# Two-layer hybrid backbone, feed-forward stages: weight halves split on GpSimd instead of ScalarE, operands and rests made on VectorE instead of GpSimd, products put in another order, and every second weight block kept in another pool of tiles

## The chip, the cores and the metric

The kernel runs on one core of a Trainium2 chip. The time is that of one execution in device microseconds (us), the median of several runs. The engines are called PE (TensorE, matmul; PEld is its weight load), DVE (VectorE), ACT (ScalarE), POOL (GpSimd) and SP (the engine that issues most DMAs). L246 is line 246 of the kernel.

## The reference, cut to what matters

```python
D_MODEL, SEQ, CTX_LEN, DEPTH, FFN_HIDDEN = 1024, 1024, 256, 2, 4096
def squared_relu_mlp(h, w1, w2):
    return jnp.square(jax.nn.relu(h @ w1)) @ w2
for l in range(DEPTH):
    need_ctx = l < DEPTH - 1
    m_lat = silu(c) @ w_mod[l] + b_mod[l]             # six rows of 1024, as m_ctx from c_ctx
    sh1, sc1, ga1, sh2, sc2, ga2 = split(m_lat, 6)
    pl = modulate(rms_norm(x, g_mix[l]), sh1, sc1) @ w_in[l]      # pc from ctx likewise
    ...                                               # four groups of mixers: SSD, RG-LRU, two attentions
    x = x + ga1 * (concat(ya, yb, yc, yd) @ w_out[l])
    x = x + ga2 * squared_relu_mlp(modulate(rms_norm(x, g_ffn[l]), sh2, sc2), w_ffn1[l], w_ffn2[l])
    if need_ctx:
        ctx = ...                                     # the same for the 256 context tokens
return x
```

All of it is float32. The latent tokens are 1024 rows, the context 256; layer 1 computes no context output.

## The kernel before, in words

Activations lie transposed: a tile holds 128 features by tokens. The tokens come in three groups, the context (256) and two latent groups of 512 (`G_CTX`, `G_LAT`). A float32 product is made of three fp32r matmuls (`mm3`, L141 to L143): high by high, high by low, low by high. So every operand is split: the high part is a rounding copy (`copy_a` on ACT, L130), the low part the difference (a subtraction on POOL, L246). Weights come through `wsplit` in halves of 128x512: SP issues the DMA of `raw` (L258, two buffers for the halves), ACT writes half of `wh`, POOL half of `wl` (three buffers each), and the next DMA into that `raw` waits for POOL.

The first feed-forward product (FFN1, 32 blocks of 128 hidden features; block `fc`) is done over two by two quarters of the latent half with seven quarter products in place of eight. `quarter` makes operands for that from the second latent group. `hidden_first` runs for an even block the context (layer 0 alone) and the first latent group, for an odd block the context alone. In the first latent group of an even block, four of eight steps of k make one quarter product; ACT copies it out of PSUM into `r` (L130) and sends it to DRAM, and then the other four steps are added in the same PSUM bank. `quarter` runs woven into `hidden_first`. `hidden_rest` takes 16 steps `q`, each with five quarter products of 12 matmuls, called `y` with w2, c21, m5, c12 and m7, c21 and c12 one step late. `weights(q)` loads two tiles `u` of 128x1024, makes sums and differences on DVE (L1300 to L1303), the high parts on ACT and the low parts on POOL (L1306, L1309). The second product (FFN2, in `ffn`) takes blocks in pairs, with 48 matmuls for each latent group and the context.

`mod_bank` computes a third of the modulation of a layer (`w_mod`, 8 MB): for each of 8 steps k two halves `raw` are loaded, and after each half two matmuls of 32 rows by 512 go to their own 32 columns of the array (L316). Bank 0 of layer 0 runs at the start, banks 1 and 2 of a layer beside its mixers (with `E` tiles, three buffers, as `land`), bank 0 of layer 1 in FFN2 of layer 0.

`weave` merges such streams by costs that the streams yield, and a scheduler then orders the instructions of each engine. Each engine runs its own in order, and waits on semaphores.

Of the kernel before, what the change touches and what calls it, by code (L numbers as in the profile page):

```python
# [93 lines left out]
class Net:  # L94
# [210 lines left out]
    def mod_bank(self, l, b, land, tag="po"):  # L305
# [3 lines left out]
        for k in range(KD):  # L309
            for hf in range(2):  # L310
                raw = f(land())[:, :1024]
                c0 = 2048 * b + 1024 * hf
                nc.sync.dma_start(raw, self.I["w_mod"][l, k * P:(k + 1) * P, c0:c0 + 1024])
                for q in range(2):
                    cg = 2 * hf + q
                    nc.tensor.matmul(ps[32 * cg:32 * cg + 32, :], self.csil[:, 2 * k:2 * k + 32], raw[:, 512 * q:512 * q + 512],  # L316
                                     start=k == 0, stop=k == KD - 1, skip_group_check=True,
                                     tile_position=(0, 32 * cg))
                yield 0.9
# [884 lines left out]
    def quarter(self, h, t, x, l, t0, rs):  # L1204
# [12 lines left out]
        def row(k):  # L1217
            a = self.S(n)
            self.stt(a, x.at(k, t0, n), p["s"][1][:, k, 0:1], rb, ALU.mult, ALU.mult)
            self.act(a, a, AF.Identity, bias=p["mods"][:, 24 + k, 0:1])  # L1220
            return a
        for k2 in range(0, 4, 2):
            rows = [(k, row(k), row(k + 4)) for k in (k2, k2 + 1)]
            yield 2.0
            for k, b12, b22 in rows:
# [4 lines left out]
                nc.gpsimd.tensor_sub(t3, b22, b12)  # L1230
# [18 lines left out]
    def hidden_first(self, l, h, groups):  # L1249


        hh, hl = h
        w1 = self.I["w_ffn1"][l]
        tags = ("pm", "qk", "qk")
        for fc in range(0, FFN // P, 1 if len(groups) == 3 else 2):
            wh, wl = self.next_weights()[0] if self.wq or self.ready else self.wcols(w1, fc * P)
            for (t0, n) in (groups[:-1] if fc % 2 == 0 else groups[:1]):
                ps = self.PS(self.pick(tags))[:, :n]
                for k in range(KD):
                    c = slice(k * P, k * P + P)  # L1260
                    self.mm3(ps, wh[:, c], wl[:, c], hh.at(k, t0, n), hl.at(k, t0, n), k == 0,
                             k in (3, KD - 1), True)
                    if k % 2:
                        yield n * 2 * 3 * 216e-3 / 512
                    if k == 3 and t0 >= CTX:
                        r = self.B()
                        self.copy_a(r, ps)
                        self.nc.scalar.dma_start(self.part[fc // 2], r)
                self.squared(self.B(n), fc, t0, n, ps)

    def hidden_rest(self, l, h, t):
# [11 lines left out]
        def weights(q):  # L1283
            raws = []
            for j in range(2):
                r = self.U()[:, :1024].rearrange("p (k c) -> p k c", k=4)
                nc.sync.dma_start(r, w1[512 * j:512 * j + 512, 256 * q:256 * q + 256].rearrange("(k p) c -> p k c", p=P))
                raws.append(r)
# [20 lines left out]
            nc.gpsimd.tensor_sub(lo[4].rearrange("p (k c) -> p k c", k=4), a(1, 1), f(h4))  # L1309
# [316 lines left out]
```

## Time and profile before

| | |
|---|---|
| median of 3 runs | 3211.46 us (3209.78 to 3217.77) |
| the profiled execution | 3211.08 us, of which the span of the trace is 3209.3 us |
| FFN1 of layer 0, from about | 845 us into the span, `hidden_first` to 1072, `hidden_rest` to 1300 |
| FFN2 of layer 0 | 1300 to 1780 us |
| FFN1 of layer 1 | `hidden_first` to 2588 us, `hidden_rest` to 2815 |
| FFN2 of layer 1 | from 2815 us |

The page gives the busy time of each engine over the span. Busy time of PE is modelled (a matmul of 128x512 shows 0.39 us, while the next one starts 0.23 us later), so its share is near 100% wherever it doesn't wait. The stages are told from the names of what is read.

### The profile page before, as it was taken

How to read it: one execution, taken by the hardware profiler on the slowest of the kernel's cores; microseconds unless marked ns; L12 is line 12 of the kernel's file. 1: busy time of each engine (PE TensorE's matmuls, PEld its weight loads, DVE VectorE, ACT ScalarE, POOL GpSimd, SP SyncE). 2: the span in 40 equal slices, each digit the busy share in tenths (PEclk: the TensorE clock that was granted, in tenths of full speed). 3: DMA queues.
4: the chain of work that ended last, by engine and by line, in shares of the span. 5: the costliest groups of instructions: out<-in, count | busy, mean ns of one | idle time of the engine just before them, and what ended most of it. 6: DMA issues, size and time to landing. Idle time of an engine off the chain costs nothing.

```text
span 3209.3 us, 46000 instructions
## 1 busy us (share of the span) xinstructions
PE 3033.6 (95%) x16354; PEld 2481.0 (77%) x16354; DVE 2078.0 (65%) x4143; ACT 1573.0 (49%) x3668; POOL 1087.8 (34%) x916
## 2 busy tenths in 40 slices
PE   6998998989978999999999999999999899999998
PEld 4788887778767777888888688787777677777776
DVE  5787777777640344677665777778787544467664
ACT  4575776666454444312111576676675644432111
POOL 2214123232584454222112512223333764522220
PEclk8999999999999999999999999999999999999999
DMA  8300012321334545633222400112322454452221
GB/s 308 93 17 24 22 36 81 128 94 42 130 122 139 177 145 168 221 128 102 86 81 64 153 18 17 27 42 85 116 79 101 147 189 149 158 175 90 95 69 70
DMA packets 239830, 335.97 MB, mean 105 GB/s; under 512 B 37360, under 2 KB 157296, under 8 KB 239600
## 3 DMA queue, kind: packets, MB, share of 16 engines
q1 hardware_dynamic: 211952, 286.88, 28.3%
q10 hardware_dynamic: 27648, 46.15, 3.9%
q8 instruction: 129, 2.11, 0.3%
q14 instruction: 101, 0.83, 0.1%
HBM read 253.28 MB, written 79.69 MB: 104 GB/s over the span
## 4 chain that ended last, share of the span: by engine, by line
PE 50%; POOL 6%; DVE 5%; DMA 4%; ACT 4%; issue 3%; POOLq 0%; ACTq 0%; SPq 0%; DVEq 0%
PE qk L141 6%; PE pm L143 6%; PE qk L143 6%; PE pm L141 5%; PE pm L142 5%; PE qk L142 5%; PE pt L143 3%; PE pt L142 3%; PE pt L141 3%; POOL wl L246 3%; DMA raw<-in_w_ffn 3%; POOL wl L1306 2%; PE pt L743 1%; PE po L316 1%; PE po L752 1%
## 5 line engine op out<-in xcount | busy, mean ns | idle before, releaser
L246 POOL TENSOR_TENSOR wl<-raw,wh 128x512 fp32r<-128x512 f32 (+1 forms) x332 | 459.0, 1395 | 1074.9 <-ACT wh L130 959.2
L130 ACT ACTIVATE wh<-raw 128x512 fp32r<-128x512 f32 (+1 forms) x332 | 203.3, 629 | 791.7 <-PE qk L142 228.2
L141 PE MATMUL pm<-u,wh 128*128 128x512 f32 (+1 forms) x1452 | 540.9, 373 | 9.9 <-ACT b L130 3.2
L143 PE MATMUL pm<-u,wl 128*128 128x512 f32 (+1 forms) x1452 | 534.8, 368 | 8.4 <-POOL wl L246 6.2
L142 PE MATMUL pm<-u,wh 128*128 128x512 f32 (+1 forms) x1452 | 532.6, 367 | 0.0
L141 PE MATMUL qk<-u,wh 128*128 128x512 f32 (+1 forms) x1152 | 433.2, 377 | 33.2 <-ACT b L130 30.8
L143 PE MATMUL qk<-u,wl 128*128 128x512 f32 (+1 forms) x1152 | 433.7, 377 | 5.8 <-POOL wl L246 3.7
L142 PE MATMUL qk<-u,wh 128*128 128x512 f32 (+1 forms) x1088 | 406.6, 374 | 1.9 <-POOL u L434 1.5
L141 PEld LDWEIGHTS pm<-u,wh 128*128 128x128 f32 x1452 | 276.7, 191 | 56.5 <-ACT b L130 5.8
L143 PEld LDWEIGHTS pm<-u,wl 128*128 128x128 f32 x1452 | 275.8, 190 | 52.4 <-POOL wl L246 11.3
L130 ACT ACTIVATE s<-pt 128x512 fp32r<-128x512 f32 (+4 forms) x548 | 251.5, 467 | 120.2 <-PE pt L743 74.0
L142 PEld LDWEIGHTS pm<-u,wh 128*128 128x128 f32 x1452 | 276.6, 191 | 38.1
L136 DVE SCALAR_TENSOR_TENSOR u<-pm,mods,u 128x512 f32<-128x512 f32 (+1 forms) x312 | 216.2, 694 | 110.9 <-PE pm L143 110.3
L141 PEld LDWEIGHTS qk<-u,wh 128*128 128x128 f32 x1152 | 219.4, 190 | 80.7 <-ACT b L130 36.1
L136 DVE SCALAR_TENSOR_TENSOR u<-qk,mods,u 128x512 f32<-128x512 f32 (+1 forms) x296 | 205.7, 695 | 113.1 <-PE qk L143 112.9
L143 PEld LDWEIGHTS qk<-u,wl 128*128 128x128 f32 x1152 | 218.6, 190 | 51.0 <-POOL wl L246 8.3
L1306 POOL TENSOR_TENSOR wl<-u,wh 128x512 fp32r<-128x512 f32 x128 | 185.7, 1475 | 168.5 <-ACT wh L130 168.5
L142 PEld LDWEIGHTS qk<-u,wh 128*128 128x128 f32 x1088 | 206.9, 190 | 41.2 <-POOL u L434 3.5
L133 ACT ACTIVATE b<-b 128x512 f32<-128x512 f32 (+4 forms) x256 | 146.7, 573 | 148.5 <-DVE b L1330 60.3
L133 ACT ACTIVATE e<-qk,t 128x512 f32<-128x512 f32 (+2 forms) x336 | 188.5, 572 | 42.3 <-DVE t L676 27.3
L1300 DVE TENSOR_TENSOR u<-u 128x512 f32<-128x512 f32 x32 | 23.7, 739 | 275.5 <-DMA u<-in_w_ffn 160.8
L747 DVE TENSOR_TENSOR s<-pt,s 128x512 fp32r<-128x512 f32 (+1 forms) x256 | 166.7, 660 | 40.5 <-ACT s L130 36.2
(318 smaller groups left out, 6935.7 us busy)
## 6 DMA issues: line engine op xcount, KB each, us to landing
raw<-in_w_ffn SPq DMA_DIRECT2D x224, 256.0 KB, 2.9
e<-in_w_mod SPq DMA_DIRECT2D x64, 512.0 KB, 4.1
u<-in_w_ffn SPq DMA_DIRECT2D x64, 512.0 KB, 4.6
m<-b ACTq DMA_DIRECT2D x96, 256.0 KB, 3.1
e<-m SPq DMA_DIRECT2D x32, 640.0 KB, 4.7
u<-in_w_mod SPq DMA_DIRECT2D x32, 512.0 KB, 5.5
e<-m SPq DMA_DIRECT2D x32, 512.0 KB, 4.4
xd<-u SPq DMA_DIRECT2D x24, 640.0 KB, 3.4
```

What stands on the lines that cost most here:

```text
L130: return self.nc.scalar.activation(o, i, AF.Copy, **k)
L133: self.nc.scalar.activation(o, i, fn, **k)
L136: self.nc.vector.scalar_tensor_tensor(o, a, s, b, op0=op0, op1=op1)
L141: mm(o, ah, bh, start=start, stop=False, skip_group_check=part)
L142: mm(o, ah, bl, start=False, stop=False, skip_group_check=part)
L143: mm(o, al, bh, start=False, stop=stop, skip_group_check=part)
L246: self.nc.gpsimd.tensor_sub(l, raw, f(h))
L316: nc.tensor.matmul(ps[32 * cg:32 * cg + 32, :], self.csil[:, 2 * k:2 * k + 32], raw[:, 512 * q:512 * q + 512], start=k == 0, stop=k == KD ...
L743: nc.tensor.transpose(pt[:, e * 256 + hd * P:e * 256 + hd * P + P], prs[hd][0][:, (i + e) * P:(i + e) * P + P], self.ident)
L747: nc.vector.tensor_sub(tl, pt[:, :w], f(th))
L752: nc.tensor.matmul(po[:, :256], V[:, kc, :], th[:, c], start=i + e == 0, stop=False)
L1306: nc.gpsimd.tensor_sub(lo[i], sr[i], f(hi[i]))
```

## The change

In `hidden_first` the high part of a weight half is written by POOL, behind the flag `act_evicts`, so that ACT has only PSUM to empty there. In `quarter` and `hidden_rest` the work of POOL goes to DVE, in `quarter` that of ACT too. In `hidden_first` of layer 0 the context product stands between the two parts of the latent product; in layer 1 the second part of a block stands behind the first part of the next even block. In `hidden_rest` the weights of step 0 go to small tiles (`S`, `R`), and m5 stands ahead of c21. In FFN2 the odd blocks' weights go to tiles of pool `U` (25 buffers). In `mod_bank` the four matmuls of a step k stand together, after both halves.

```diff
@@ split
-        self.copy_a(h, raw)
+        if self.act_evicts:
+            self.nc.gpsimd.tensor_copy(h, raw)
+        else:
+            self.copy_a(h, raw)
         self.nc.gpsimd.tensor_sub(l, raw, f(h))
@@ mod_bank
-                for q in range(2):
-                    cg = 2 * hf + q
-                    nc.tensor.matmul(ps[32 * cg:32 * cg + 32, :], self.csil[:, 2 * k:2 * k + 32], raw[:, 512 * q:512 * q + 512],
...
-                yield 0.9
+                raws.append(raw)
+
+            for cg in range(4):
+                nc.tensor.matmul(ps[32 * cg:32 * cg + 32, :], self.csil[:, 2 * k:2 * k + 32],
+                                 raws[cg // 2][:, 512 * (cg % 2):512 * (cg % 2) + 512],
...
+            yield 1.8
@@ quarter
-            self.act(a, a, AF.Identity, bias=p["mods"][:, 24 + k, 0:1])
+            nc.vector.tensor_scalar(a, a, p["mods"][:, 24 + k, 0:1], None, op0=ALU.add)
...
-                nc.gpsimd.tensor_sub(t3, b22, b12)
+                sub(t3, b22, b12)
...
-                    self.copy_a(oh, raw)
-                    nc.gpsimd.tensor_sub(ol, raw, f(oh))
+                    nc.vector.tensor_copy(oh, raw)
+                    sub(ol, raw, f(oh))
@@ hidden_first
+            if fc % 2 == 0:
+                t0, n = G_LAT[0]
+                ps = self.PS(self.pick(tags))
+                yield from part(ps, w, t0, n, range(4))
+                r = self.B()
+                self.copy_a(r, ps)
+                nc.scalar.dma_start(self.part[fc // 2], r)
+
+                if len(groups) == 3:
+                    yield from context(fc, w)
+                    yield from second(fc, w, ps)
+                else:
+                    if last:
+                        yield from second(*last)
+                    last = fc, w, ps
+            else:
+                yield from context(fc, w)
@@ hidden_rest, weights(q)
+                raws = {}
+                for i, j in ((0, 1), (1, 1), (0, 0), (1, 0)):
+                    r = (self.S() if j else self.R(512)).rearrange("p (k c) -> p k c", k=4)
...
+                sr = [self.S() for _ in range(4)]
...
-                nc.gpsimd.tensor_sub(lo[i], sr[i], f(hi[i]))
+                nc.vector.tensor_sub(lo[i], sr[i], f(hi[i]))
@@ hidden_rest, steps
             m5, m7, c21, c12 = front(q)
+            m5()
             if last:
                 last[0]()
-            m5()
-            if last:
                 last[1]()
             m7()
@@ ffn
+        self.act_evicts = True
         weave((pending, 30), (self.hidden_first(l, h, groups), 90 * len(groups) - 90))
+        self.act_evicts = False
...
-            ws = [self.wrows(w2, fc * P) for fc in fs]
+            ws = [self.wrows(w2, fc * P, self.U if fc % 2 else None) for fc in fs]
@@ layer, n2
                 rs = yield from self.norm_stats(x, *g)
+                yield 1.5
                 yield from self.quarter(h2, t2, x, l, g[0], rs)
```

The rows below show ACT before, in `hidden_first` of layer 0: the high parts of two halves of one block (`wh` from `raw`), among the activations that empty PSUM (`qk`, `pm`) and their DMAs to DRAM.

```order
L130 ACTIVATE wh_10784<-raw_10785 128x512
L133 ACTIVATE b_10665<-qk_10637 128x512
L130 ACTIVATE wh_10784<-raw_10789 128x512
L133 ACTIVATE b_10665<-b_10665 128x512
L133 ACTIVATE b_10704<-pm_10679 128x256
L1247 DMA m28_10061<-b_10665 128x512
L133 ACTIVATE b_10704<-b_10704 128x256
L133 ACTIVATE s_11546<-s_11546,mods0_340 128x512
L1247 DMA m29_10062<-b_10704 128x256
L130 ACTIVATE wh_10825<-raw_10826 128x512
L133 ACTIVATE b_10747<-qk_10718 128x256
```

With the change POOL has these rows for two blocks, an odd one and the even one behind it (CAST is the copy that rounds, of L246; L249 is the subtraction).

```order
L246 CAST wh_10780<-raw_10781 128x512
L246 CAST wh_10780<-raw_10785 128x512
L249 TENSOR_TENSOR wl_10779<-raw_10781,wh_10780 128x512
L249 TENSOR_TENSOR wl_10779<-raw_10785,wh_10780 128x512
L246 CAST wh_10819<-raw_10820 128x512
L249 TENSOR_TENSOR wl_10818<-raw_10820,wh_10819 128x512
L246 CAST wh_10819<-raw_10824 128x512
L249 TENSOR_TENSOR wl_10818<-raw_10824,wh_10819 128x512
```

The copies moved from ACT to POOL; an odd block has both copies ahead of both subtractions, an even block alternates. This pattern stands through layer 0; in layer 1 the last 11 blocks all have both copies first.

The next rows are DVE before, in `hidden_rest` of layer 0, one step (`b` and `s` from PSUM `qk` and `pm` or `pt` are the sums that end a product; `u` from `u` are the weights of a later step).

```order
L1326 TENSOR_TENSOR b_12328<-qk_12326,b_12324 128x512
L1330 TENSOR_TENSOR b_12218<-qk_12220,b_12218 128x512
L1300 TENSOR_TENSOR u_12624<-u_12616,u_12618 128x512
L1301 TENSOR_TENSOR u_12624<-u_12624,u_12616 128x512
L1338 TENSOR_TENSOR b_12222<-pm_12221,b_12222 128x512
L1302 TENSOR_TENSOR u_12625<-u_12616 128x512
L1303 TENSOR_TENSOR u_12625<-u_12618,u_12624 128x512
L1343 TENSOR_TENSOR s_12329<-qk_12326,b_12324 128x512
L1344 TENSOR_TENSOR s_12329<-pt_12327,s_12329 128x512
```

And DVE with the change, one step (L1351 and L1354 are the low parts).

```order
L1371 TENSOR_TENSOR b_12546<-qk_12544,b_12542 128x512
L1351 TENSOR_TENSOR wl_12628<-u_12626,wh_12630 128x512 x2
L1345 TENSOR_TENSOR u_12838<-u_12834,u_12836 128x512
L1346 TENSOR_TENSOR u_12838<-u_12838,u_12834 128x512
L1375 TENSOR_TENSOR b_12436<-qk_12438,b_12436 128x512
L1383 TENSOR_TENSOR b_12440<-pm_12439,b_12440 128x512
L1351 TENSOR_TENSOR wl_12629<-u_12627,wh_12631 128x512 x2
L1388 TENSOR_TENSOR s_12547<-qk_12544,b_12542 128x512
L1347 TENSOR_TENSOR u_12839<-u_12834 128x512
L1389 TENSOR_TENSOR s_12547<-pt_12545,s_12547 128x512
L1354 TENSOR_TENSOR s_12632<-u_12624,s_12633 128x512
L1348 TENSOR_TENSOR u_12839<-u_12836,u_12838 128x512
```

DVE has 14 instructions in a step where it had 9, the five low parts among them.

## Rows read from the trace of the kernel before

**Rows 1.** The page, part 1: busy time of each engine, share of the span, instructions.

```profile
PE 3033.6 (95%) x16354; PEld 2481.0 (77%) x16354; DVE 2078.0 (65%) x4143; ACT 1573.0 (49%) x3668; POOL 1087.8 (34%) x916
```

**Rows 2.** Windows: stretch, length, busy time of each engine, granted clock, DMA share, GB/s.

```profile
871.00:963.00 92.00, 73.80 (x444) 65.03 (x443) 34.92 (x30) 48.13 (x96) 73.10 (x53) 0.94 0.41 126
963.00:1072.00 109.00, 99.25 (x610) 87.98 (x609) 0.00 (x0) 46.34 (x92) 40.04 (x32) 0.98 0.48 148
1072.00:1090.00 18.00, 13.27 (x51) 9.81 (x50) 11.50 (x13) 7.76 (x14) 12.95 (x9) 0.91 0.72 231
1090.00:1292.00 202.00, 198.60 (x842) 157.22 (x841) 93.25 (x125) 93.52 (x154) 101.28 (x72) 1.00 0.49 156
1300.00:1780.00 480.00, 473.40 (x2441) 391.47 (x2440) 332.90 (x510) 99.87 (x196) 104.09 (x77) 1.00 0.33 112
2588.00:2600.00 12.00, 9.22 (x31) 6.44 (x30) 6.73 (x8) 5.83 (x11) 8.03 (x6) 0.86 0.88 301
```

**Rows 3.** Waits of PE, 871 to 1072: us in total, times, longest.

```profile
PE qk L141 <- ACT b L130: 25.5, 13, 5.8
```

**Rows 4.** Timeline in FFN1: ACT, PE where it starts a second part, POOL (layer 1).

```profile
915.60 0.63 ACT L130 ACTIVATE wh<-raw 128x512 fp32r<-128x512 f32 x1 [7.86 <-DMA raw<-in_w_ffn]
919.64 0.80 PE L141 MATMUL qk<-u,wh 128*128 128x512 f32 x1 [5.79 <-ACT b L130]
...
965.32 0.50 PE L141 MATMUL qk<-u,wh 128*128 128x512 f32 x1 [1.65 <-ACT b L130]
...
1055.73 0.50 PE L141 MATMUL qk<-u,wh 128*128 128x512 f32 x1 [0.91 <-ACT b L130]
...
2579.27 2.54 POOL L246 TENSOR_TENSOR wl<-raw,wh 128x512 fp32r<-128x512 f32 x2
```

**Rows 5.** Chain of work that ended last: pieces of a weight half's way, both layers.

```profile
871.62 1.31 POOL wl L246
...
984.62 4.96 DMA raw<-in_w_ffn
...
1067.31 6.01 DMA u<-in_w_ffn
...
2515.83 3.15 POOL wl L246 x2
```

**Rows 6.** Groups by shape: POOL 963 to 1072, then POOL 871 to 963.

```profile
L246 POOL TENSOR_TENSOR wl<-raw,wh 128x512 fp32r<-128x512 f32 x32 | 41.1, 1294 | 61.6 <-ACT wh L130 61.3
...
L1240 POOL TENSOR_TENSOR u<-s,u 128x512 fp32r<-128x512 f32 x16 | 23.6, 1499 | 0.9 <-ACT u L130 0.9
```

**Rows 7.** DMA issues, 872 to 1067: size, median us to landing.

```profile
raw<-in_w_ffn SPq DMA_DIRECT2D x58, 256.0 KB, 3.1
```

**Rows 8.** Groups of POOL's instructions by shape, whole span.

```profile
L929 POOL TENSOR_TENSOR s<-s,we 128x128 f32<-128x128 f32 x80 | 31.1, 418 | 31.9 <-ACT s L130 31.5
L413 POOL TENSOR_TENSOR t<-t,mhalf 128x4 f32<-128x4 f32 x8 | 8.1, 1015 | 25.4 <-DVE t L411 25.4
```

**Rows 9.** Timeline of PE in `hidden_rest`: the first matmul of c21, two neighbouring steps.

```profile
1104.73 0.50 PE L141 MATMUL qk<-u,s 128*128 128x512 f32 x1 [0.25 <-DVE s L1343]
...
1119.21 0.49 PE L141 MATMUL qk<-u,s 128*128 128x512 f32 x1 [0.28 <-DVE s L1343]
```

**Rows 10.** Groups of DVE by shape in `hidden_rest` of layer 0, 1090 to 1292.

```profile
L1301 DVE TENSOR_TENSOR u<-u 128x512 f32<-128x512 f32 x14 | 20.8, 1487 | 0.4
L1330 DVE TENSOR_TENSOR b<-qk,b 128x512 f32<-128x512 f32 x14 | 9.7, 692 | 21.4 <-PE qk L143 21.3
```

**Rows 11.** Timeline of PE: modulation matmuls beside a mixer, and in FFN2.

```profile
101.17 1.05 PE L316 MATMUL po<-e,csil 128*32 128x512 f32 x4
...
1338.22 1.07 PE L316 MATMUL po<-u,csil 128*32 128x512 f32 x8
```

**Rows 12.** Timeline of PE in FFN1 of layer 0: matmuls that wait for nothing.

```profile
966.13 0.40 PE L141 MATMUL qk<-u,wh 128*128 128x512 f32 x1
966.36 0.39 PE L142 MATMUL qk<-u,wh 128*128 128x512 f32 x1
```

More of the change, by code (lines that the diff above doesn't have):

```diff
@@ L309, in mod_bank @@
         for k in range(KD):
+            raws = []
             for hf in range(2):
@@ L313, in mod_bank @@
                 nc.sync.dma_start(raw, self.I["w_mod"][l, k * P:(k + 1) * P, c0:c0 + 1024])
[L314 to L319 removed]
+                raws.append(raw)
+            for cg in range(4):
+                nc.tensor.matmul(ps[32 * cg:32 * cg + 32, :], self.csil[:, 2 * k:2 * k + 32],
+                                 raws[cg // 2][:, 512 * (cg % 2):512 * (cg % 2) + 512],
+                                 start=k == 0, stop=k == KD - 1, skip_group_check=True,
+                                 tile_position=(0, 32 * cg))
+            yield 1.8
         sb = self.B()
@@ L1249, in hidden_first @@
     def hidden_first(self, l, h, groups):
+        nc = self.nc
         hh, hl = h
@@ L1254, in hidden_first, with part @@
         tags = ("pm", "qk", "qk")
-        for fc in range(0, FFN // P, 1 if len(groups) == 3 else 2):
[L1256 to L1269, printed above, removed]
+        def part(ps, w, t0, n, ks):
+            for k in ks:
+                c = slice(k * P, k * P + P)
+                self.mm3(ps, w[0][:, c], w[1][:, c], hh.at(k, t0, n), hl.at(k, t0, n), k == 0, k in (3, KD - 1), True)
+                if k % 2:
+                    yield n * 2 * 3 * 216e-3 / 512
@@ new lines, in context, with second @@
+        def context(fc, w):
+            t0, n = G_CTX
+            ps = self.PS(self.pick(tags))[:, :n]
+            yield from part(ps, w, t0, n, range(KD))
+            self.squared(self.B(n), fc, t0, n, ps)
+        def second(fc, w, ps):
+            t0, n = G_LAT[0]
+            yield from part(ps, w, t0, n, range(4, KD))
+            self.squared(self.B(), fc, t0, n, ps)
+        last = None
+        for fc in range(0, FFN // P, 1 if len(groups) == 3 else 2):
+            w = self.next_weights()[0] if self.wq or self.ready else self.wcols(w1, fc * P)
+            if fc % 2 == 0:
+                t0, n = G_LAT[0]
+                ps = self.PS(self.pick(tags))
[12 more added lines that the diff above has]
+                yield from context(fc, w)
@@ L1271, in hidden_rest @@
+        if last:
+            yield from second(*last)
     def hidden_rest(self, l, h, t):
@@ L1283, in weights @@
         def weights(q):
[L1284 to L1288, printed above, removed]
+            if q:
+                raws = []
+                for j in range(2):
+                    r = self.U()[:, :1024].rearrange("p (k c) -> p k c", k=4)
+                    nc.sync.dma_start(r, w1[512 * j:512 * j + 512, 256 * q:256 * q + 256].rearrange("(k p) c -> p k c", p=P))
+                    raws.append(r)
+                su = [self.U(), self.U()]
+                sr = [su[i // 2][:, 512 * (i % 2):512 * (i % 2) + 512] for i in range(4)]
+            else:
+                raws = {}
+                for i, j in ((0, 1), (1, 1), (0, 0), (1, 0)):
+                    r = (self.S() if j else self.R(512)).rearrange("p (k c) -> p k c", k=4)
+                    nc.sync.dma_start(r, w1[512 * j:512 * j + 512, i * P:i * P + P].rearrange("(k p) c -> p k c", p=P))
+                    raws[i, j] = r
+                sr = [self.S() for _ in range(4)]
             def a(i, j):
-                return raws[j][:, :, i * P:i * P + P]
+                return raws[j][:, :, i * P:i * P + P] if q else raws[i, j]
             wl = [self.W()[:, :1024], self.W()[:, :1024]]
             wh = [self.wp.tile([P, 4 * WU], F32R, tag="wh", name="wh", bufs=3)[:, :1024] for _ in range(2)]
-            su = [self.U(), self.U()]
-            lo, hi, sr = ([y[i // 2][:, 512 * (i % 2):512 * (i % 2) + 512] for i in range(4)] for y in (wl, wh, su))
+            lo, hi = ([y[i // 2][:, 512 * (i % 2):512 * (i % 2) + 512] for i in range(4)] for y in (wl, wh))
             lo.append(self.S(n, F32R))
```

3 lines of the change are left out of this document (2 added, 1 removed).

## The prediction

> **What bounds the kernel now.** I read the page first: PE is busy 95% of the span and no other engine over 65% [rows 1], so what can be won is PE's idle time and its own work. Then the windows, stage by stage [rows 2]. In the first 92 us of FFN1 of layer 0 PE is busy 73.8 us, in the next 109 us 99.3, between `hidden_first` and `hidden_rest` 13.3 of 18 at a granted clock of 0.91, in `hidden_rest` 198.6 of 202, in FFN2 473.4 of 480. FFN1 of layer 0 is the sick stage. The waits of PE say why: 25.5 us in 13 waits for ACT's copy of the first part out of PSUM [rows 3]. The timeline shows why that copy is late: ACT stands 7.86 us in front of a weight half that hasn't landed, and PE then waits 5.79 us for the copy queued behind it [rows 4]. The chain of waits shows what lies under that, a loop: POOL's subtraction frees `raw`, the next DMA lands 3 to 5 us later, ACT, POOL, and again [rows 5].
>
> Matmuls of 128x512 that wait for nothing start 0.23 us apart [rows 12]; one of 256 columns I take at half. A pair of blocks in layer 0 then needs 24 x 0.23 + 48 x 0.115 = 11.04 us; between 965.32 and 1055.73 seven pairs took 90.4 us, 12.9 each [rows 4].
>
> **FFN1 of layer 0.** The wait for the copy goes: 24 context matmuls (2.76 us) now stand between the parts, longer than ACT's 0.57 us and its way. But POOL gets the copies, and both `raw` buffers now turn on POOL alone. Their price, c, no row shows (POOL never copies). Bounds: 0.42 us, the 128x128 subtraction, a quarter of the elements [rows 8], and 1.29 us, the 128x512 subtraction, which reads two inputs [rows 6]. The two subtractions give 0.42 = a + 128 b and 1.29 = a + 512 b, so b = 2.27 ns and a = 0.13 us; with half the slope for half the inputs c = 0.13 + 512 x 1.13 ns = 0.71, and with the wait between two instructions I take 0.75.
>
> GPSIMD Engine Reference of the Trainium skill (4.1 Engine selection) advises against elementwise work there, as about twice slower for two inputs, and says that one input is roughly line rate; section 3.1 gives 769 ns for 512 elements in its best loop. DVE's 0.69 us [rows 10] against POOL's 1.29 [rows 6] agrees with the first. An estimate by 0.77 would move the sum below by under 2 us.
>
> The loop for an odd block (copy, copy, subtract, subtract, as the order of POOL shows) and an even one (copy, subtract, copy, subtract): a landing takes 3.1 us [rows 7], and longer if its DMA was issued just behind another (4.96 is such a one [rows 5]); I take 3.8 for these, between the two and nearer to the first. From the odd block's second copy at 0: copy to 0.75, first subtraction to 2.05, its DMA lands at 5.15; second subtraction to 3.35, lands at 7.15. Even block: copy 5.2 to 5.95, subtraction to 7.25, second copy to 8.0, subtraction to 9.3. Issued at 7.25 and 9.3, the next odd block's halves land at 10.35 and 12.4, and its second copy starts there. So 12.4 us a pair, 6.2 a block: more than PE's 5.5, less than the 6.45 of now. With c = 0.42 it is 11.75, with 1.29 14.1.
>
> 29 blocks (58 DMAs [rows 7]) pass from 871.62 [rows 5]: 29 x 6.2 = 180 us. While `quarter` runs on DVE, both slow each other: now POOL's subtractions take 1.50 there, and a DVE subtraction beside POOL 1.49, against 1.29 and 0.69 alone [rows 6, 10]. At c = 0.9 and 1.5 for a subtraction the pair takes about 13.4 (6 instructions of it on the loop, 0.35 us more on each kind, three each), 0.5 a block over some 13 blocks: 7 us. The last block ends at 871.6 + 180 + 7 = 1058, PE within its own 2.8 us, minus what lies beside: 1058 against 1072 now. **Minus 14.**
>
> **The way into hidden_rest, layer 0.** Now PE loses 4.7 us and clock in 18 us, since the weights of step 0 wait for tiles (the DMA of 6.01 us issued at 1067 [rows 5]). With small tiles the last load is issued at the last block's first subtraction: landing 3.1, DVE 0.7, ACT 0.63, 4.6 us with the ways between, of which PE covers some 2.8. What is left is about 2 of 7 (4.7 and the low clock). **Minus 5.** In layer 1 36 matmuls (8.3 us) stand behind that subtraction and all is hidden: of 2.8 us idle and the clock of 0.86 in 12 us [rows 2] **minus 4.**
>
> **hidden_rest.** A step takes 14.48 us [rows 9], its 60 matmuls 13.8 to 13.9. c21 waits for DVE's sum, 0.25 us with a restart, 0.45 lost in all. m5 ahead of c21 gives that sum 2.8 us more. DVE gets 5 x 0.69 = 3.5 us a step: 14 instructions x 0.69 = 9.7, 70% of a step, without POOL beside it (L1301 now takes 1.49 for the same shape [rows 10]). What is late next: w2 of the step after waits for a weight buffer until c12 is through. From there ACT's 0.63 and DVE's 0.69 with ways make 1.6, and m7 covers 2.8; the sum for c21 is through some 7.5 us after that point, needed at 8.3. Without that cover a step would lose a microsecond, 16 in a layer. I take the gain, 16 x 0.5 in each layer. **Minus 16.**
>
> **FFN2.** Odd blocks in `U` tiles load ahead; now low parts come late, 6.6 us idle in layer 0 [rows 2], about 0.2 us in each of 15 pairs in layer 1. The cost is nothing as long as 25 tiles hold 8 of x, 8 of two pairs' activations, 4 weights and up to 4 of modulation. **Minus 6 and minus 3.**
>
> **FFN1 of layer 1.** No context lies beside, each pair of halves serves 5.5 us of PE, and the last 11 blocks have both copies first: second copy at 0, subtractions to 3.35, landing 3.8 later, 7.2 us a block against (2579 - 2515.8)/10 = 6.3 now, with 2515.8 from [rows 5] and 2579 the last such piece [rows 4]. Ten blocks lose 9 us; I take half, since PE's backlog covers a part, and a little for the buffer that the deferred part frees 2.8 us later: **plus 5.**
>
> **Modulation.** A visit of PE costs 1.05 us whether two matmuls run beside each other or four (each leaves two records) [rows 11]. The order of PE has 15, 17, 14 and 15 visits for the four banks beside mixers before, 15, 12, 12 and 11 after: 11 to 12 fewer, 12 us of PE's time. Of three `E` tiles two are now held at once, and a second half lands over 4 us after the visit that frees its tile, so I take half. **Minus 6** (bounds -12 and +5).
>
> **Sum.** -14 - 5 - 4 - 16 - 9 + 5 - 6 = -49 from the profiled 3211.1 (span 3209.3 and 1.8 around it, 0.4 under the median): **3162 us.**
>
> **The rivals.** *The loop is slower than I make it* (24%): copies as dear as subtractions, or DVE and POOL shutting each other out in `quarter` as 1.49 and 1.50 hint. 14.1 a pair is 0.85 a block, 24 us in layer 0, and 6 in layer 1: 3192.
>
> *Loads are no limit* (13%): landings of 2.8 and cheap copies keep three `wh` buffers filled. FFN1 of layer 0 then falls to PE's own time: 871 to 1072 has 18.2 + 9.8 us idle [rows 2] and a clock of 0.94 and 0.98, about 8 us more; with 4 lost at its ends that is -40 in place of -14, and -6 in place of +5 in layer 1: 3125. For it: ACT's way now shows it, against it: the landing of 5 us in the chain.
>
> *The change gives back what it takes* (8%): the slow loop, and nothing from `hidden_rest` or modulation because DVE blocks behind ACT: 3192 + 16 + 6 = 3214, within 0.3% (9.6 us, about what a measurement here can tell from no change).
>
> *The copy on POOL is far dearer* (7%), the one that ends slower: POOL takes 1.02 us for 128x4 [rows 8], so not all it does goes by elements. Each microsecond of c adds 1.5 a block, about 42 in layer 0, and 10 in layer 1; from c = 0.75 + 59/52 = 1.9 the kernel is slower by 0.3%. At 2.5 it is 3162 + 91 = 3253.
>
> *As forecast* 48%, 3144 to 3180. Faster by over 0.3% then holds 0.85, within 0.08, slower 0.07. The range leaves out half of the fast end below 3120 and nearly all above 3202.
>
> **What would show it.** CAST on POOL in FFN1 of layer 0 at 0.6 to 0.9 us; PE's wait for ACT there gone and one for POOL (or PE's start after L249) in its place, some 1.3 us a pair; pairs 12.4 apart late in the stage; its end near 1058 less what the stages before give; layer 1's blocks 7 apart; no wait for DVE in `hidden_rest` at 13.9 to 14.0 a step; low parts no longer awaited in FFN2. Wrong would make it: CAST outside 0.4 to 1.3, a wait of PE for `w_mod` of microseconds, or a step of `hidden_rest` that DVE ends.

## The result, and the profile after

The changed kernel takes 3180.48 us (median of 4 runs, 3170.66 to 3183.80), the kernel before 3210.62 beside it; the ratio is 0.9897 with an interval of 0.987 to 0.9924. So it is faster by 0.8 to 1.3%, inside the range of 3120 to 3202 that the prediction names, and 18 us above the forecast of 3162. The profiled execution took 3178.89 us, its span 3177.1.

The sum landed close because two errors met, which is luck. The stages, between rows of VectorE's timeline that both traces have (the copy `t<-pt` in the statistics of the FFN's norm for the first group, and the first and last sums of a product's output in FFN2), with what the prediction gave to each:

| stretch | before | after | measured | forecast |
|---|---|---|---|---|
| up to the norm ahead of FFN1, layer 0 | 830.7 | 830.4 | -0.3 | -3 (modulation) |
| that norm and FFN1, layer 0 | 481.3 | 466.9 | -14.4 | -27 |
| FFN2 of layer 0, to the next norm | 447.3 | 437.6 | -9.7 | -6 |
| layer 1 up to its second norm | 718.1 | 712.1 | -6.0 | -3 (modulation) |
| norm and FFN1, layer 1 | 351.5 | 361.5 | +10.0 | -7 |
| FFN2, layer 1 | 362.3 | 358.9 | -3.4 | -3 |
| from its last sum to the end of the span | 18.2 | 9.7 | -8.5 | 0 |

The prediction's 6 us for the modulation are halved here between the two layers, as the visits saved are (5 and 6). The fourth stretch took 711 to 717 us in the experiments, 716.1 in the one with the modulation of before, so its -6.0 can't be told from nothing. Both FFN1 stages together gave 4.4 us where 34 were forecast; FFN2 and the end of the kernel gave 12.6 more than forecast.

Part 1 of the page after, and windows that answer to [rows 1] and [rows 2]: PE is busy all of `hidden_rest` and of FFN2 now, and the sick stretches are the first of FFN1 and the 20 us around the way into `hidden_rest`, at a granted clock of 0.83.

```profile
PE 3006.2 (95%) x16354; PEld 2485.1 (78%) x16354; DVE 2200.5 (69%) x4407; ACT 1490.0 (47%) x3520; POOL 869.3 (27%) x800
```

```profile
871.00:963.00 92.00, 77.24 (x475) 68.52 (x474) 63.26 (x83) 23.94 (x49) 70.42 (x52) 0.93 0.40 125
963.00:1055.00 92.00, 88.50 (x553) 77.33 (x551) 0.00 (x0) 24.84 (x51) 57.52 (x63) 1.00 0.51 159
1055.00:1075.00 20.00, 12.84 (x61) 10.92 (x61) 8.08 (x13) 6.46 (x13) 2.37 (x2) 0.83 0.55 176
1075.00:1277.00 202.00, 201.87 (x870) 163.07 (x869) 130.46 (x206) 95.38 (x160) 0.00 (x0) 1.00 0.52 169
1297.00:1735.00 438.00, 438.00 (x2295) 367.58 (x2295) 310.01 (x474) 83.52 (x164) 88.22 (x65) 1.00 0.33 108
```

The waits of PE from 850 to 1066 us. The 25.5 us in 13 waits for ACT's copy [rows 3] are gone; two long waits stand there, each a single one.

```profile
PE pm L143 <- POOL wl L249: 12.3, 1, 12.3
PE qk L141 <- ACT b L130: 7.2, 1, 7.2
PE qk L143 <- POOL wl L249: 4.7, 8, 0.9
PE qk L142 <- POOL u L443: 3.5, 3, 1.6
```

The first, in the timeline of POOL: a copy that takes 0.61 us elsewhere takes 15.80, and PE waits for the low part queued behind it.

```profile
902.94 0.62 POOL L246 CAST wh<-raw 128x512 fp32r<-128x512 f32 x1 [1.31 <-DMA raw<-in_w_ffn]
905.09 15.80 POOL L246 CAST wh<-raw 128x512 fp32r<-128x512 f32 x1 [1.53 <-DMA raw<-in_w_ffn]
920.85 2.96 POOL L249 TENSOR_TENSOR wl<-raw,wh 128x512 fp32r<-128x512 f32 x2
```

DVE at the same time. From 904.33 to 920.3 its instructions follow each other without a gap, and each is a copy or reads two tensors of SBUF; 29 of them start while POOL's copy stands. POOL's copy ends inside the first one that isn't (L136 at 920.33 reads one tensor of SBUF, `u`, and the PSUM tile `pt`).

```profile
904.33 0.68 DVE L1238 TENSOR_TENSOR s<-s,u 128x512 f32<-128x512 f32 x1
904.93 0.68 DVE L1239 TENSOR_TENSOR s<-s 128x512 f32<-128x512 f32 x1
905.54 0.68 DVE L1240 TENSOR_TENSOR s<-s,u 128x512 f32<-128x512 f32 x1
906.14 0.41 DVE L1248 CAST u<-s 128x512 fp32r<-128x512 f32 x1
...
919.99 0.41 DVE L1248 CAST u<-s 128x512 fp32r<-128x512 f32 x1
920.33 0.73 DVE L136 SCALAR_TENSOR_TENSOR s<-u,ms,pt 128x512 f32<-128x512 f32 x1
920.99 1.66 DVE L1249 TENSOR_TENSOR u<-s,u 128x512 fp32r<-128x512 f32 x1
```

The second is the way into `hidden_rest`. ACT's order has the high part of step 0's weights (`wh<-s`, L130) ahead of the copy of the last first part out of PSUM (`b<-qk`); the former waits for a load that is issued only when POOL frees `raw`, the latter was ready some 9 us earlier (PE's last matmul of that part starts at 1051.81), and PE waits for it. Behind this pause PE's matmuls start 0.43 us apart for some 3.5 us, where 0.23 is usual: the lower of the two levels of its clock (1.2 and 2.4 GHz), part of the 0.83 above.

```profile
1048.76 0.33 ACTq L1256 DMA_DIRECT2D m<-b  x1
1061.03 0.63 ACT L130 ACTIVATE wh<-s 128x512 fp32r<-128x512 f32 x1 [12.31 <-DVE s L1345]
1061.57 0.58 ACT L130 ACTIVATE b<-qk 128x512 f32<-128x512 f32 x1
```

In layer 1 there is more of that kind. POOL's timeline in the norm: a copy stands ahead of the norm's products (L443) and waits 4.01 us for a `wh` buffer, another copy and two subtractions stand between the first of them and the second, and PE waits 3.17 us for the second; 20 us later the norm's sum L412 comes late behind copies and subtractions, and PE waits 4.46 us for the sum on DVE that it feeds. Before, PE's waits at these two places were 1.19 and 0.91 us.

```profile
2452.24 0.62 POOL L246 CAST wh<-raw 128x512 fp32r<-128x512 f32 x1 [4.01 <-PE pt L142]
2452.81 1.30 POOL L443 TENSOR_TENSOR u<-s,u 128x512 fp32r<-128x512 f32 x1
2454.06 1.75 POOL L249 TENSOR_TENSOR wl<-raw,wh 128x512 fp32r<-128x512 f32 x1
2455.76 0.60 POOL L246 CAST wh<-raw 128x512 fp32r<-128x512 f32 x1
2456.44 1.29 POOL L249 TENSOR_TENSOR wl<-raw,wh 128x512 fp32r<-128x512 f32 x1
2457.66 1.75 POOL L443 TENSOR_TENSOR u<-s,u 128x512 fp32r<-128x512 f32 x1
```

```profile
2459.46 0.80 PE L142 MATMUL qk<-u,wh 128*128 128x512 f32 x1 [3.17 <-POOL u L443]
2482.16 1.84 PE L418 MATMUL pt<-one,s 128*128 128x1 f32 x8 [4.46 <-DVE s L414]
```

And SP's queue from 2530 to 2575: the DMA of step 0's weights into an `S` tile (L1332) waits 8.4 us for `quarter` to give the tile back, and the loads of `raw` (L264) stand behind it. They go out at 2544.01, though POOL's last use of the first `raw` ended at 2539.92; then their copy is shut out for 4.8 us as above. PE waits 7.3 us.

```profile
SPq L264 <- POOL wl L249: 17.4, 6, 6.7
SPq L1332 <- DVE s L1239: 8.4, 1, 8.4
```

### The profile page after: what moved, and what is told of

Read it like the earlier page. It is cut to its first block, busy times and chain, and to the rows that moved or that the text cites. A ratio compares the mean times of both kernels' runs of the same rounds, so it can differ in the third digit from the quotient of the medians.

```text
span 3177.1 us, 45882 instructions
## 1 busy us (share of the span) xinstructions
PE 3006.2 (95%) x16354; PEld 2485.1 (78%) x16354; DVE 2200.5 (69%) x4407; ACT 1490.0 (47%) x3520; POOL 869.3 (27%) x800
## 4 chain that ended last, share of the span: by engine, by line
PE 63%; DVE 11%; DMA 7%; ACT 6%; POOL 6%; issue 5%; SPq 0%; ACTq 0%; POOLq 0%; DVEq 0%
PE pm L143 7%; PE pm L141 7%; PE pm L142 7%; PE qk L142 6%; PE qk L141 6%; PE qk L143 6%; DMA raw<-in_w_ffn 3%; PE pt L142 3%; PE pt L141 3%; PE pt L143 3%; PE pt L752 3%; DVE u L136 3%; POOL wl L249 2%; PE po L761 2%; DMA u<-in_w_ffn 2%
## 5 line engine op out<-in xcount | busy, mean ns | idle before, releaser
L249 POOL TENSOR_TENSOR wl<-raw,wh 128x512 fp32r<-128x512 f32 (+1 forms) x268 | 378.9, 1427 | 1216.5 <-ACT wh L130 899.6
L141 PE MATMUL pm<-u,wh 128*128 128x512 f32 (+1 forms) x1270 | 476.1, 375 | 11.8 <-POOL wh L246 7.3
L143 PE MATMUL pm<-u,wl 128*128 128x512 f32 (+1 forms) x1270 | 469.4, 370 | 13.9 <-POOL wl L249 13.8
L142 PE MATMUL pm<-u,wh 128*128 128x512 f32 (+1 forms) x1270 | 467.9, 369 | 0.0
L141 PE MATMUL qk<-u,wh 128*128 128x512 f32 (+1 forms) x876 | 328.8, 376 | 12.4 <-ACT b L130 10.8
L143 PE MATMUL qk<-u,wl 128*128 128x512 f32 (+1 forms) x876 | 330.6, 377 | 9.4 <-POOL wl L249 9.2
L130 ACT ACTIVATE wh<-raw 128x512 fp32r<-128x512 f32 (+1 forms) x176 | 106.1, 628 | 447.4 <-PE qk L142 177.8
L142 PE MATMUL qk<-u,wh 128*128 128x512 f32 (+1 forms) x812 | 303.8, 374 | 7.1 <-POOL u L443 6.6
L130 ACT ACTIVATE s<-pt 128x512 fp32r<-128x512 f32 (+4 forms) x548 | 251.5, 467 | 120.7 <-PE pt L752 75.0
L141 PEld LDWEIGHTS pm<-u,wh 128*128 128x128 f32 x1270 | 244.5, 193 | 49.5 <-POOL wh L246 7.7
L136 DVE SCALAR_TENSOR_TENSOR u<-pm,mods,u 128x512 f32<-128x512 f32 (+1 forms) x312 | 215.6, 692 | 91.2 <-PE pm L143 90.1
L142 PEld LDWEIGHTS pm<-u,wh 128*128 128x128 f32 x1270 | 244.3, 193 | 31.0
L136 DVE SCALAR_TENSOR_TENSOR u<-qk,mods,u 128x512 f32<-128x512 f32 (+1 forms) x296 | 204.8, 692 | 85.9 <-PE qk L143 85.3
L141 PEld LDWEIGHTS qk<-u,wh 128*128 128x128 f32 x876 | 167.0, 191 | 44.8 <-ACT b L130 11.7
L1425 DVE TENSOR_TENSOR u<-e,u 128x256 fp32r<-128x256 f32 (+1 forms) x160 | 159.1, 1011 | 46.1 <-ACT u L130 23.8
L142 PEld LDWEIGHTS qk<-u,wh 128*128 128x128 f32 x812 | 154.8, 191 | 36.8 <-POOL u L443 8.5
L141 PE MATMUL pm<-wh,u 128*128 128x256 f32 (+1 forms) x592 | 176.8, 299 | 2.0 <-ACT b L133 1.7
```

The source lines that it names most:

```text
L130: return self.nc.scalar.activation(o, i, AF.Copy, **k)
L136: self.nc.vector.scalar_tensor_tensor(o, a, s, b, op0=op0, op1=op1)
L141: mm(o, ah, bh, start=start, stop=False, skip_group_check=part)
L142: mm(o, ah, bl, start=False, stop=False, skip_group_check=part)
L143: mm(o, al, bh, start=False, stop=stop, skip_group_check=part)
L1425: self.nc.vector.tensor_sub(al[:, t], raw[:, t], f(ah[:, t]))
```

## The experiments

All were timed beside the kernel before, in three sets in which it took 3208.20, 3206.61 and 3205.95 us (3210.62 beside the changed kernel), so a few us between runs of different sets say nothing. q_gap, late_copies, act_copies and ffn2_last_small, the first set, change one thing in the changed kernel.

**q_gap**: a tiny copy out of PSUM breaks VectorE's chain in `quarter`.

```diff
                     nc.vector.tensor_copy(oh, raw)
                     sub(ol, raw, f(oh))
+                    nc.vector.tensor_copy(self.tiny(4, "gap"), rb[:, 0:4])
```

> The changed kernel with one small VectorE copy of 128x4 out of PSUM behind each pair of copy and subtraction in quarter (20 in a layer, 0.16 us each), and nothing else. Theory A: the GpSimd copy of 15.8 us at 905 us (alone 0.61) and the one of 4.8 us at 2548 were shut out by VectorE, whose 25 and 13 instructions there followed each other without a gap and all copied or read two operands from SBUF; one that reads PSUM lets GpSimd in, as the one at 920.3 did. Then no GpSimd copy is longer than 4 us, PE's 12.5 us pause in FFN1 of layer 0 falls under 2, the 7.4 us pause of layer 1 to about 4 (the late issue of the load stays), and the time is about 3179 - 11 - 3 = 3165 us. Rival B: VectorE has nothing to do with it (the long copy waits for its operands, or the engine stood still for another reason): the pauses stay, 3179 us or a little above.

3164.42 us (3163.00 to 3166.82), ratio 0.9865 (0.9852 to 0.9878): 16 us under the changed kernel by the medians, and each run is under its fastest (3170.66). Theory A holds. No POOL instruction of FFN1 is longer than 2 us. The groups by shape over `hidden_first` of layer 0 give 702 ns on average for the copies, where the changed kernel has 920:

```profile
L249 POOL TENSOR_TENSOR wl<-raw,wh 128x512 fp32r<-128x512 f32 x58 | 80.0, 1390 | 2.2
L246 POOL CAST wh<-raw 128x512 fp32r<-128x512 f32 x58 | 40.7, 702 | 57.4 <-DMA raw<-in_w_ffn 51.6 <-PE qk L142 1.8 <-PE pm L143 1.5
```

FFN1 of layer 0 is 9.7 us shorter than in the changed kernel (457.1), that of layer 1 7.4 (354.1). The pause of 7.5 us ahead of `hidden_rest` of layer 0 stays. One thing does not fit the simplest reading: the copy in the place of the long one (905.29 here) had its turn after one subtraction and took 0.91 us, ahead of the first tiny copy at 911.02. So the tiny copy did not free that one; what ties the stops to the chain is their count over all builds, behind gap2_act.

**late_copies** and **act_copies**: ScalarE writes the high parts for the early blocks, or for all.

```diff
# late_copies, in hidden_first's loop
+            self.act_evicts = fc >= (16 if len(groups) == 3 else 22)
# act_copies, in ffn
-        self.act_evicts = True
+        self.act_evicts = False
```

> The changed kernel with the high parts of FFN1's weights written by ScalarE for blocks under 16 (layer 0) and under 22 (layer 1), by GpSimd from there on. Theory A: GpSimd's copies cost where VectorE runs quarter (12.5 us in layer 0, 3 in layer 1) and where they stand ahead of the norm's work in GpSimd's queue (3.3 and 4.6 us of PE at 2456 and 2477), and pay only in the late blocks. Then about 3179 - 12 - 3 - 6 = 3158 us, with at most 3 us back from waits for ScalarE. Rival B: ScalarE's copies stand ahead of the copy out of PSUM again as before the change, and PE waits for it some 1.5 us a pair in eight pairs: 3179 - 20 + 12 = 3171. Rival C: the subtractions on GpSimd are shut out by VectorE as the copy was, 3175 to 3180.

> The changed kernel with all high parts of FFN1's weights on ScalarE as before the change, everything else as changed. Theory A: GpSimd's copies pay in the late blocks of layer 0 (11.9 us a pair against 12.9), about 8 us with the waits for the copy out of PSUM, and cost 20 us elsewhere: about 3179 - 20 + 8 = 3167 us. Rival B: with the context's matmuls between the two parts a late copy out of PSUM is hidden, and GpSimd's copies pay nothing: 3158. Rival C: without them the waits for ScalarE of before (25 us in layer 0) come back for the most part: 3185 or more.

3190.57 us (3188.70 to 3197.56) and 3186.49 us (3173.84 to 3190.62). For the first my theory and its time fell: it is slower than the changed kernel, and the reason is that of rival C, whose time was 10 us too low. For the second the time is that of C, but not its reason. What is shut out now is POOL's subtractions, longer than the copy was: in the first of the two, two pairs in layer 0, and in layer 1 four subtractions take 8 us on average, two of them 14.7 each (alone 1.29).

```profile
917.38 10.58 POOL L249 TENSOR_TENSOR wl<-raw,wh 128x512 fp32r<-128x512 f32 x2 [4.22 <-ACT wh L130]
929.85 1.26 POOL L249 TENSOR_TENSOR wl<-raw,wh 128x512 fp32r<-128x512 f32 x1 [1.88 <-ACT wh L130]
931.53 1.28 POOL L249 TENSOR_TENSOR wl<-raw,wh 128x512 fp32r<-128x512 f32 x1 [0.42 <-ACT wh L130]
937.49 14.45 POOL L249 TENSOR_TENSOR wl<-raw,wh 128x512 fp32r<-128x512 f32 x2 [4.68 <-ACT wh L130]
```

```profile
L249 POOL TENSOR_TENSOR wl<-raw,wh 128x512 fp32r<-128x512 f32 x4 | 31.9, 7984 | 9.6 <-ACT wh L130 9.6
```

The two runs below join the broken chain of q_gap with the edits of these two. act_copies is 6 us slower than the changed kernel by the medians, with intervals that overlap; while DVE shuts POOL out, neither run says what the copies on POOL cost by themselves. The joined ones, **gap_act** and **gap_late**, do.

> The kernel with the small copies out of PSUM in quarter (3164 us), and all high parts of FFN1's weights on ScalarE again. Theory A, after the runs before this: the long waits of the version with ScalarE's copies (PE paused 6.6 and 9.9 us in layer 0, 13.3 and 13.7 in layer 1) are GpSimd's subtractions shut out by VectorE (9.0, 12.2, 14.7 and 15.0 us long, alone 1.3). With VectorE's chain broken they go too, and what is left is what GpSimd's copies give or take: 3186 - 6 - 9 - 12 - 12 = 3147 us, so the copies on GpSimd cost about 17 us, in the norm's work queued behind them and at the end of FFN1. Rival B: GpSimd's copies pay once VectorE lets GpSimd in: 3170 or more, with PE's waits for ScalarE's copy out of PSUM in the late pairs.

> The kernel with the small copies out of PSUM in quarter, and the high parts on ScalarE for blocks under 16 (layer 0) and 22 (layer 1), on GpSimd behind them. Theory A: the pauses of 6.9, 10.7, 13.3 and 13.3 us go, since they were subtractions shut out: 3190 - 40 = 3150 us, and the pause of 7.5 us at the end of FFN1 of layer 0 stays, since GpSimd's copies end it as in the changed kernel. Rival B: 3164, no better than with all copies on GpSimd.

3142.48 us (3140.64 to 3144.72), ratio 0.9798 (0.9784 to 0.9811), and 3152.84 us (3152.12 to 3156.10), ratio 0.9831 (0.9818 to 0.9845). Theory A holds in both. With the chain broken, the copies on GpSimd cost 22 us (3164.4 against 3142.5), 19 of them in FFN1; the second keeps them for the late blocks and still loses 10. FFN1 of layer 0 takes 446.8 us with ScalarE's copies and 457.1 with GpSimd's, that of layer 1 345.3 and 354.1. In the late pairs of layer 0 the DMAs of the first parts follow each other every 11.5 us with ScalarE's copies (seven distances, 11.1 to 11.9), every 11.9 in the changed kernel (five, 11.7 to 12.3); the way into `hidden_rest` costs PE 1.2 us instead of 7.5, and the waits behind copies in the norm of layer 1 are gone. The wait that the copies on GpSimd were to remove is gone with ScalarE's copies too, since the context's matmuls stand between the parts; what is left of PE's waits for ScalarE from 850 to 1060 is

```profile
PE qk L141 <- ACT b L130: 6.2, 6, 3.4
PE pm L141 <- ACT wh L130: 1.9, 1, 1.9
```

One subtraction of gap_act, at 2491.76 in layer 1, still took 4.8 us. DVE's timeline there shows the tiny copy at work: seven instructions without a gap, then the copy of 0.15 us, and from there DVE's own next subtraction takes 1.63 us, having to wait for POOL in its turn.

```profile
2491.42 0.68 DVE L1238 TENSOR_TENSOR s<-s,u 128x512 f32<-128x512 f32 x1
...
2494.16 0.68 DVE L1249 TENSOR_TENSOR u<-s,u 128x512 fp32r<-128x512 f32 x1
2494.77 0.68 DVE L1242 TENSOR_TENSOR s<-u,s 128x512 f32<-128x512 f32 x1
2495.37 0.15 DVE L1250 COPY gap<-pt 128x4 f32<-128x4 f32 x1
2495.48 1.63 DVE L1243 TENSOR_TENSOR s<-s,u 128x512 f32<-128x512 f32 x1
```

**gap2_act** puts the same line behind the third and the last of the six sums as well.

```diff
                 sub(t1, t1, b11l)
+                nc.vector.tensor_copy(self.tiny(4, "gap"), rb[:, 0:4])
...
                 add(t4, t4, b21l)
+                nc.vector.tensor_copy(self.tiny(4, "gap"), rb[:, 0:4])
```

> The version with ScalarE's copies and the small copies out of PSUM in quarter (3142 us), with two more of them in each of the four rows, behind the third and the last of the six sums, where one subtraction on GpSimd still took 4.8 us and PE paused 3.4. Theory A: that pause falls under 1.5, nothing else moves: 3142 - 2 to 3 = about 3140 us. Rival B: the pause comes from the load, no change.

3140.44 us (3135.25 to 3144.41), ratio 0.9792 (0.9777 to 0.9806). The pause of 3.4 us is gone and FFN1 of layer 1 takes 341.3 us, but the time can't be told from gap_act's. These two are the fastest versions, 2% under the kernel before and over 1% under the changed one.

The stops of all builds together show the cause better than one run. With VectorE's chain unbroken (the changed kernel, late_copies, act_copies, ffn2_last_small) the profiled executions have twelve POOL instructions of over 2.5 us in `hidden_first`, of 4.8 to 15.8 us. Each ends 0.4 to 1.3 us, about its own time, behind the start of an L136, which reads PSUM (six), or behind a pause or the end of VectorE's chain (six). The eight builds with the tiny copy have eight, of 3.0 to 5.2 us, and each ends so behind the start of a tiny copy. No run put another short instruction there, such as a copy from SBUF to SBUF: whether it must read PSUM is not shown.

**quarter_back_act**: ScalarE's copies, and `quarter` as before the change.

```diff
-            nc.vector.tensor_scalar(a, a, p["mods"][:, 24 + k, 0:1], None, op0=ALU.add)
+            self.act(a, a, AF.Identity, bias=p["mods"][:, 24 + k, 0:1])
...
-                    nc.vector.tensor_copy(oh, raw)
-                    sub(ol, raw, f(oh))
+                    self.copy_a(oh, raw)
+                    nc.gpsimd.tensor_sub(ol, raw, f(oh))
```

> The changed kernel with the weights' high parts on ScalarE and quarter as before the change (its copies on ScalarE, its subtractions on GpSimd), so that of the changes in FFN1 only the new order of the products is left, beside those of hidden_rest, FFN2 and the modulation. Theory A: VectorE works in quarter only now and then, so nothing is shut out, but GpSimd has 22 us of subtractions more in each layer in the stretch where the loads wait for it: about 8 us more in each than the version with the broken chain and ScalarE's copies (3142): 3155 to 3160 us. Rival B: moving quarter gave nothing, 3142 to 3146. Rival C: it is what saved FFN1, 3170 or more.

3157.52 us (3155.85 to 3159.75), ratio 0.9846 (0.9833 to 0.9860). Theory A holds: `quarter` on VectorE is worth 15 us once its chain is broken (3142.5), and without the break it costs 29 (3186.5 for act_copies). FFN1 takes 457.3 and 351.1 us here, 446.8 and 345.3 with `quarter` on VectorE, and no POOL instruction in it is longer than 2 us.

The other four measure the rest of the sum. Three start from q_gap, one from the changed kernel.

**gap_rest_back**: m5 behind c21, and the low parts in `hidden_rest` on GpSimd.

```diff
-            m5()
             if last:
                 last[0]()
+            m5()
+            if last:
                 last[1]()
...
-                nc.vector.tensor_sub(lo[i], sr[i], f(hi[i]))
+                nc.gpsimd.tensor_sub(lo[i], sr[i], f(hi[i]))
```

> The kernel with the small copies out of PSUM in quarter, and hidden_rest as before the change in two points: m5 behind c21, low parts on GpSimd (the tiles of step 0 stay). Theory A: the prediction's step, 0.45 us in each of 16 steps in two layers, comes back: 3164 + 14 = 3178 us, PE waits for VectorE ahead of c21 in most steps. Rival B: the gain of hidden_rest has another cause, 3164 to 3168.

3182.25 us (3176.24 to 3183.47): 18 us back, where 14 were expected. The waits of PE over `hidden_rest` of layer 0 show the cause; in the changed kernel there is no such wait.

```profile
PE qk L141 <- DVE s L1389: 4.1, 12, 0.9
```

Layer 0 accounts for 6.7 us of FFN1's time; layer 1 for 17.0, of which some lies ahead of `hidden_rest` (two copies on POOL of 4.9 and 4.0 us). By PE's starts a step of `hidden_rest` is 0.43 us longer in layer 0 and 0.53 in layer 1, 15 us in 32 steps. The run takes the order and the low parts back together, so it does not tell the two apart.

**gap_start_U**: step 0's weights in large tiles again.

```diff
-            if q:
+            if True:
                 raws = []
...
-                return raws[j][:, :, i * P:i * P + P] if q else raws[i, j]
+                return raws[j][:, :, i * P:i * P + P]
```

> The kernel with the small copies out of PSUM in quarter, and the weights of hidden_rest's step 0 in large tiles as before the change. Theory A: the small tiles cost more than they give, since ScalarE's copies of these weights stand in its queue ahead of a copy out of PSUM and wait for a load that is issued only when GpSimd frees the tile (pauses of 7.5 and 4.5 us between hidden_first and hidden_rest); with large tiles the pause is 5 us in layer 0 as before the change and 3 in layer 1: 3164 - 4 = 3160 us. Rival B: the small tiles give what was predicted (5 and 4 us): 3173.

3159.51 us (3155.63 to 3168.70), ratio 0.9855 (0.9837 to 0.9872), against q_gap's 0.9865. That excludes B's 3173 and does not tell A from no difference: in layer 0 the pause on the way into `hidden_rest` is 7.0 us instead of 7.5 (A had 5), in layer 1 2.0 instead of 4.5.

**ffn2_last_small** and **gap_ffn2**: the last odd block of FFN2, or all odd blocks, back in the small-weight pool.

```diff
-            ws = [self.wrows(w2, fc * P, self.U if fc % 2 else None) for fc in fs]
+            ws = [self.wrows(w2, fc * P, self.U if fc % 2 and fc < NF - 2 else None) for fc in fs]
```

> The changed kernel with only the last odd block of FFN2 of each layer back in the small-weight pool. Theory A: the 8.5 us gained behind the last accumulation (18.2 us to the end of the span before, 9.7 now) came from that pool, whose tiles also hold the output rows on their way out; with the last block's low part back in it the output waits again: about 3179 + 6 to 9 = 3187 us. Rival B: the end is shorter for another reason (the order of PE there), 3179 us, at most 1 us more for the last pair's low part.

> The kernel with the small copies out of PSUM in quarter and GpSimd's copies (3164 us), with the odd blocks of FFN2 back in the small-weight pool. Theory A: from the stages of the changed kernel, 9.7 us in FFN2 of layer 0, 3.4 in layer 1 and 5 to 8 at the end come back: 3164 + 19 = 3183 us. Rival B: what FFN2 of layer 0 gained came from the modulation beside it, and only 6 to 12 come back: 3173.

3184.72 us (3181.66 to 3191.28) and 3186.74 us (3184.20 to 3188.03). The second is 22 us above q_gap, where A gave 19. By stages it is 13.4 in FFN2 of layer 0 (451.0 against 437.6; PE waits 8.9 us for low parts there, in q_gap not at all), 2.9 in layer 1, and 9.2 at the end (18.8 against 9.7); the other stretches differ by -4.6 to +0.9 in the two profiled executions. The first shows what belongs to the last block's tiles: its last stretch is 18.4 us, but the sums before it end 3.7 us earlier, so that they are worth 5 us in the profiled executions and 4 by the medians, less than the 6 to 9 that A gave. The output rows on their way out lie in tiles of the pool `wl` (`o` in `store_out`); with the pool full of weights PE's transposes wait. The waits of PE from 3185 to 3210 before, then from 3150 to 3180 in the changed kernel:

```profile
PE po L1516 <- DVE wl L1518: 2.5, 3, 0.8
PE po L1516 <- ACT wl L130: 2.0, 3, 0.7
```

```profile
PE po L1563 <- DVE wl L1565: 1.6, 2, 1.0
```

**gap_mods**: `mod_bank` as in the lines that the diff of the change takes out, two matmuls behind each half.

> The kernel with the small copies out of PSUM in quarter and GpSimd's copies (3164 us), with the modulation's matmuls after each half again. Theory A: PE is held by other waits where they stand beside the mixers, so of the 12 us of visits saved the stages show nothing in layer 0 and up to 6 in FFN2 and layer 1: 3164 + 3 = 3167 us. Rival B, as predicted: 3170. Rival C: the new order costs more than it saves, since two of three tiles are held at once: 3160.

3165.44 us (3160.95 to 3169.99), ratio 0.9874 (0.9857 to 0.9892): no difference that these runs can tell, 1 us by the medians.

## Why the prediction held, and where it did not

**The step that failed** is the one on `quarter` in FFN1 of layer 0, "both slow each other", 0.15 us on a copy and 0.21 on a subtraction, 7 us in all; for layer 1 the prediction has no such term. The runs show another thing: an instruction of POOL is held for as long as DVE's chain goes on, 15.8 us at one place in layer 0 and 4.8 at one in layer 1. q_gap, which adds work to VectorE and takes 16 us away, and the stops of all builds show the cause. By its own sign of being wrong, a CAST outside 0.4 to 1.3 us, these two copies fall outside. The rival of the slow loop named DVE and POOL shutting each other out, but priced it as a longer pair of blocks everywhere (24 us), not as one long stop.

**The price of the copy** was 0.75 us; 32 copies between 963 and 1057 took 0.613 on average. (The 769 ns of GPSIMD Engine Reference of the Trainium skill, 3.1, is above that too.) The loop came out at 11.9 us a pair against 12.4. Both were right in kind, and q_gap has FFN1 of layer 0 3 us from the forecast (-24.1 against -27). POOL's last subtraction there ended at 1057.4 in the changed kernel, where 1058 was forecast, but by luck: the long stop and the shorter loop cancel. PE was through with `hidden_first` only at 1069.5.

**The way into hidden_rest** was forecast at -5 and -4. In layer 0 PE lost 5.6 us in pauses before (2.58, 2.13, 0.36 and 0.52 by its timeline) and loses 7.7 now; in layer 1 it waits 3.7 us where it waited 1.4. The small tiles were counted for the load alone, not for what their copies hold up in ScalarE's queue. In layer 0 they are not what the pause hangs on: it is 7.0 us with large tiles (gap_start_U), and 1.2 with ScalarE's copies (gap_act).

**FFN1 of layer 1** was forecast at +5 for its first part, and -7 in all; it came to +10. What was left out is the work of the norm in POOL's queue behind the copies (3.2 and 4.5 us of PE, 1.2 and 0.9 before) and the `S` tile on SP (7.3 us with the copy shut out behind it). Both were there to be read in the orders of POOL and SP with the change.

**hidden_rest** is right: 60 matmuls at 0.2305 us make 13.83; in layer 0 PE's starts leave 0.57 us over that in a step before (8.3 us in 14.6 steps) and 0.13 after (2.0 in 15.3), 7 us in the layer; in layer 1 it is 0.49 and 0.16, 5 us. The forecast was 8 in each.

**FFN2** is right in kind, with 9.7 us where 6 were forecast; of the 8.5 us at the end nothing was forecast, since no sentence asks who else takes tiles from the pool that the odd blocks leave.

**Modulation** was priced at 6 us; gap_mods gives 1, with runs that spread over 9. Beside the mixers the visits became fewer (32 to 27 in layer 0, 29 to 23 in layer 1) at 1.1 us each, but the stretches with the mixers took no longer in gap_mods (827.9 and 716.1 us) than in q_gap (830.9 and 716.8); what took up the time saved stays open.

The sum was thus 30 us too low in FFN1 and 13 too high elsewhere. The aim of the change, to free ScalarE by GpSimd's copies, costs 22 us once VectorE's chain is broken. Its gains are those of `quarter` on VectorE, `hidden_rest` and FFN2, and in layer 0 the new order of the products: with it and without the moves of copies and `quarter` (quarter_back_act) FFN1 is 24 us shorter than before there, 7 of them in `hidden_rest`, but 0.4 in layer 1.

One sum of the prediction is wrong without bearing on the result: the rival that loads are no limit adds the 4 us lost at the ends where they go off, 18.2 + 9.8 + 8 - 4 = 32 in place of 40, so its time is 3133 and not 3125.

## What to carry to other kernels

Before moving elementwise work onto GpSimd, or a long run of it onto VectorE, look whether the two will work at once: a chain of VectorE instructions without a gap can hold GpSimd for all of its length, and an instruction of 0.15 us that reads PSUM, put between them, kept the stops to 5.2 us and gave the time back. An instruction that waits for a load or a buffer holds everything behind it on its engine or DMA queue, so a copy that is moved has to be looked at in the order of its new engine: here a norm, a copy out of PSUM and a weight load came late for it. When a pool is relieved, ask who else draws from it; here output rows, some 5 us at the end.

## What was not expected of the hardware

SBUF — State Buffer of the Trainium skill ("Who interferes with whom") says that VectorE, in a two-port mode or with two inputs in SBUF, and GpSimd share a pair of ports as an exclusive lock, and that the one that starts first has it for the whole instruction while the other blocks. The runs agree that the other blocks, but not only for one instruction: the copy at 905.09 stood behind 29 more of VectorE's, and subtractions of 8.9 to 14.7 us in late_copies did the same. At other places of the same stage GpSimd got its turn after one (a VectorE subtraction of 1.09 or 1.78 us beside copies of 0.7 to 1.0). What decides between the two stays open, and so does why the changed kernel's runs spread over 13 us (3170.7 to 3183.8) and those of q_gap over 4; gap_start_U, with the tiny copies, spreads over 13 too.
